# Column-group modulation in the mixers of layer one: two blocks per unit with split contraction, or four blocks per unit with whole contraction

## The chip, the cores and the metric

The kernel runs on one core of a Trainium2 chip. The metric is the device time of one execution in microseconds (us). TensorE (PE) multiplies, ScalarE (ACT) and VectorE (DVE) evict, cast and normalise, SyncE (SP) issues nearly all DMAs, in order, on one queue.

## The reference, cut to what matters

Two layers of a diffusion trunk run over 128 context and 256 denoising tokens. Each layer is modulated by a vector computed from a condition; there are two conditions, one per group of tokens.

```python
mod = jax.nn.silu(cond) @ P['mod_w'][l] + P['mod_b'][l]
sh1, sc1, g1, sh2, sc2, g2 = jnp.split(mod[:, None, :], 6, axis=-1)
h = _rms(x, P['norm1_g'][l]) * (1 + sc1) + sh1
...
x = x + g1 * (merged @ P['w_out'][l])
h = _rms(x, P['norm2_g'][l]) * (1 + sc2) + sh2
```

`mod_w` is 1024 x 6144, so `mod` has 48 blocks of 128 channels: blocks 0 to 15 are `sh1` and `sc1`, 16 to 23 `g1`, 24 to 39 `sh2` and `sc2`, 40 to 47 `g2`. The change concerns blocks 16 to 39 of the first layer, which are needed only after that layer's mixers.

## The kernel before, in words

Weights stay in HBM in pieces of at most 128 x 1024 numbers (512 KB). `raw` (line 179) loads a piece into a tile `wr`; there are four `wr` buffers, shared by all pieces. `split` turns a piece into two rounded halves, `wh` by a cast on ScalarE (line 194) and `wl` by a subtraction on VectorE (line 195), of which there are four and three buffers. The `wr` buffer is free again once the subtraction has read it. Each product is then three matmuls on TensorE (lines 201, 202, 203); two of them need `wh`, one needs `wl`.

A modulation unit (`mod_unit`) uses its pieces as loaded, in full fp32, so their two `wr` buffers are free only when TensorE has read them. Each half of the contraction is one piece of four blocks of 128 rows by 256 columns. Line 362 puts the four row blocks on the four groups of 32 columns of the array, so that the four run side by side and each group of 32 PSUM partitions holds a quarter of the sum. ScalarE copies that out (line 365), TensorE transposes it twice (line 370), VectorE adds the four quarters (372) and the bias (375). In the first layer's mixers 12 such units make blocks 24 to 39 and then 16 to 23.

`dense` yields the projections one by one and calls `unit(1)` between them at 18 places, of which the first 12 issue one unit each. `weave` interleaves the dense part with the attention (`sc`, `ta`, `av`, `tw` tiles) by a count of steps. The tile scheduler then fixes each engine's order before the run; loads are hoisted by a priority of 400 instructions.

Of the kernel before, what the change touches and what calls it, by code (L numbers as in the profile page):

```python
# [17 lines left out]
ALU = mybir.AluOpType  # L18
# [3 lines left out]
P = 128  # L22
D = 1024
KD = 8
# [20 lines left out]
PV = {}  # L45
# [17 lines left out]
AB = 3  # L63


MODS = ((0, 1, 8, 8), (2, 2, 1, 4), (3, 1, 8, 8))


def weight_pieces():

    out = []

    def add(key, name, l, nkb, cols, per):
        for i, k0 in enumerate(range(0, nkb, per)):
            out.append(((l, *key, i), name, l, range(k0, min(k0 + per, nkb)), cols))

    def r(a, n):
        return list(range(a, a + n))

    def mod(l, s):  # L80
        for p in range(MODS[s][3]):
            a = MODS[s][0] * D + MODS[s][1] * p * P
            add(("mod", s, p), "mod_w", l, KD, r(a, P) + r(a + MODS[s][2] * P, P), 4)

    mod(0, 0)
    for l in range(L):
        for i in range(1 if l == 0 else AB):
            add(("u", i), "w_in", l, KD, r(512 + P * i, P) + r(P * i, P), 4)
        for c in range(2):
            for i in range(3):  # L90

                e = r(3200, 32) if (i, c) == (2, 1) else []
                add(("qkv", i, c), "w_in", l, KD, r(1024 + 512 * i + 256 * c, 256) + e, 3 if e else 4)
        add(("c", 0), "w_in", l, KD, r(2560, 256), 4)
        add(("c", 1), "w_in", l, KD, r(2816, 256), 4)
        add(("c", 2), "w_in", l, KD, r(3072, P), 8)
        for i in range(1 if l == 0 else AB, 4):
            add(("u", i), "w_in", l, KD, r(512 + P * i, P) + r(P * i, P), 4)
        for g in range(2):
            add(("uq", g), "w_uq", l, 3, r(384 * g, 384), 2)  # L100
            add(("ukv", g), "w_ukv", l, 2, r(512 * g, 512), 2)
            for i in range(4):
                add(("g", 1 + g, i), "w_in", l, KD, r(3232 + 1024 * (1 + g) + 256 * i, 256), 4)
            for i in range(4):
                n, w = (("od", "w_diff_out"), ("om", "w_mla_out"))[g]
                add((n, i), w, l, 4, r(256 * i, 256), 4)
        if l == 0:
            mod(0, 2)
            mod(0, 1)
        for i in range(4):  # L110
            add(("g", 0, i), "w_in", l, KD, r(3232 + 256 * i, 256), 4)
            add(("oc", i), "w_conv_out", l, 4, r(256 * i, 256), 4)
        for i in range(4):
            add(("wo", i), "w_out", l, KD, r(256 * i, 256), 4)
        for f in range(2):
            for i in range(8):
                add(("up", f, i), "w_up", l, KD, r(2048 * f + 256 * i, 256), 4)
            for i in range(4):
                for j, k0 in enumerate(range(16 * f, 16 * f + 16, 4)):
                    out.append(((l, "dn", f, i, j), "w_down", l, range(k0, k0 + 4), r(256 * i, 256)))  # L120
    return out


PIECES = weight_pieces()
WOFF = {}
_o = 0
# [18 lines left out]
class Body:  # L145
# [204 lines left out]
    def mod_cols(s, p):  # L350

        a, d = MODS[s][0] * KD + MODS[s][1] * p, MODS[s][2]
        return slice(a, a + d + 1, d)

    def mod_unit(self, l, s, p, pool=None):

        V, E = self.V, self.E
        ps = self.psum("mm" if pool is None or p % 2 else "av")
        for h in range(2):
            w, _, n = self.raw((l, "mod", s, p, h), pool)  # L360
            for j in range(4):
                E.matmul(ps[32 * j : 32 * j + 32, :256], self.cond[:, 4 * h + j, :], w[:, j * 256 : j * 256 + 256],  # L362
                         start=h == 0, stop=h == 1, tile_position=(0, 32 * j))
        m = self.tl(pool, [P, 256], "m", 5) if pool else self.slot("tmpA", 256)
        self.A.copy(m, ps[:, :256])

        def rest():
            pt = self.psum("tw")
            for i in range(2):
                E.transpose(pt[:, i * P : i * P + P], m[:, i * P : i * P + P], self.ident)  # L370
            t = self.tl(self.cp, [P, 2, 2], "modt", 2)
            V.tensor_reduce(t, pt[:, : 2 * P].rearrange("p (i j c) -> p i c j", i=2, j=4)[:, :, 0:2, :], AX.X, ALU.add)
            b = self.mod_cols(s, p)
            o = PV["modb"][0]
            V.tensor_tensor(self.modT[l][:, b, :], t, self.pv[l][:, o + b.start : o + b.stop : b.step]
                            .unsqueeze(2).to_broadcast([P, 2, 2]), ALU.add)

        if pool:
            return rest
        self.after(4, rest)  # L380

    def mod_block(self, l, b):
# [818 lines left out]

    def dense(self, l, h, m):

        units = [(s, p) for s in (2, 1) for p in range(MODS[s][3])] if l == 0 else []

        def unit(n):
            for _ in range(n):
                if units:
                    self.mod_unit(0, *units.pop(0))
                    yield 4  # L1210

        yield from self.qkv(l, h, 0)
        yield from self.qkv(l, h, 1)
        yield from self.cproj(l, h)
        todo = list(range(2 if l == 0 else AB, CB))
        yield from self.conv_in(l, todo.pop(0), h)
        yield from unit(1)
        yield from self.mla_q(l, 0)
        for b in todo:
            yield from self.conv_in(l, b, h)  # L1220
            yield from unit(1)
        if l == 0:
            yield from self.mla_kv(l, 0)
        for i in range(4):
            m += yield from self.gate(l, 1, i, h)
            yield from unit(1)
            if l > 0 and i == 0:
                yield from self.mla_kv(l, 0)
            if i == (1 if l == 0 else 2):
                yield from self.mla_q(l, 1)  # L1230
            if i == (2 if l == 0 else 3):
                yield from self.mla_kv(l, 1)
        yield "od1"
        for i in range(4):
            yield from self.branch_out(l, "od", i, self.od, m[2 * i : 2 * i + 2], None)
            yield from unit(1)
        self.flags.add("od")
        gm = []
        for i in range(4):
            gm += yield from self.gate(l, 2, i, h)  # L1240
            yield from unit(1)
        yield "om1"
        self.conv(l)
        for i in range(4):
            yield from self.branch_out(l, "om", i, self.om, gm[2 * i : 2 * i + 2], m)
            if i == 0:
                self.flags.add("z")
            yield from unit(1)
        yield from unit(len(units))
        yield "oc"  # L1250

    def chains(self, l):
# [168 lines left out]
```

## Time and profile before

| | |
|---|---|
| median of 3 runs | 1370.95 us (1370.3 to 1371.1) |
| profiled execution | 1370.67 us |
| its span, first to last instruction | 1368.9 us |
| TensorE busy in the span | 1350.6 us (99%) |
| VectorE, ScalarE busy | 1065.6 us (78%), 686.8 us (50%) |
| mean granted TensorE clock | 0.997 of full speed |
| first layer's mixers with the 12 units | about 150 to 330 us of the span |

The span leaves out 1.8 us around the profiled execution. Busy TensorE time counts each matmul to its modelled end, and neighbours overlap: what a matmul costs is the distance between starts, not its length. A record of an fp32 matmul is one of its two passes, so a unit's 8 matmuls are 16 records; a transpose is one record.

### The profile page before, as it was taken

The page shows a single profiled execution, that of the slowest core. Times are in us where ns is not written, and L with a number is a line of the kernel's source. Part 1 is how long each engine was busy: PE and PEld are TensorE (multiplying, and loading weights), DVE is VectorE, ACT ScalarE, POOL GpSimd, SP SyncE. Part 2 cuts the span into 40 slices and gives each one's busy share as a digit, 9 for nine tenths or more (in the row PEclk, how much of TensorE's full clock was granted, in tenths as well). Part 3 has the DMA queues.
Part 4 walks back from the last instruction along what each step waited for, and adds up shares of the span by engine and source line. Part 5 has one row for each costly group of instructions (what it writes and reads, how often), then busy time and mean ns, then how long its engine had stood idle before and what let it go on. Part 6 is the DMA issues. An engine that isn't in the chain of part 4 may idle for free.

```text
span 1368.9 us, 22037 instructions
## 1 busy us (share of the span) xinstructions
PE 1350.6 (99%) x8192; PEld 1267.4 (93%) x8192; DVE 1065.6 (78%) x2549; ACT 686.8 (50%) x1297; POOL 16.7 (1%) x34
## 2 busy tenths in 40 slices
PE   5999999999999999999999999999999999999998
PEld 3999887879999999999999998988899999999998
DVE  5777998995998999975568779989999897435532
ACT  3556656453544662276336566664544466326621
POOL 0000000000000000000000000000000000000000
PEclk9999999999999999999999999999999999999999
DMA  9523344445574677753444323322257454333341
GB/s 371 172 91 112 121 141 146 138 171 211 157 250 137 202 223 247 240 166 123 149 146 139 104 89 104 93 81 88 80 201 250 147 184 155 124 124 123 126 144 53
DMA packets 62683, 209.46 MB, mean 153 GB/s; under 512 B 7840, under 2 KB 13600, under 8 KB 62320
## 3 DMA queue, kind: packets, MB, share of 16 engines
q1 hardware_dynamic: 56304, 196.93, 43.8%
q0 software_dynamic: 1808, 6.63, 1.5%
q10 hardware_dynamic: 4464, 4.50, 0.9%
q8 instruction: 64, 1.05, 0.3%
q14 instruction: 43, 0.35, 0.1%
HBM read 203.54 MB, written 4.49 MB: 152 GB/s over the span
## 4 chain that ended last, share of the span: by engine, by line
PE 95%; DVE 2%; DMA 1%; ACT 1%; SPq 0%; issue 0%; DVEq 0%
PE mm L201 20%; PE mm L202 19%; PE mm L203 19%; PE sc L202 9%; PE sc L203 9%; PE sc L201 9%; PE sc L755 3%; PE av L967 2%; PE ta L770 1%; PE mm L362 1%; DMA wr<-wts 1%; PE av L822 1%; PE tw L936 1%; DVE wl L195 1%; PE tw L921 0%; ACT wh L194 0%
## 5 line engine op out<-in xcount | busy, mean ns | idle before, releaser
L194 ACT CAST wh<-wr 128x1024 fp32r<-128x1024 f32 (+3 forms) x280 | 289.5, 1035 | 346.0 <-PE mm L202 173.8
L195 DVE TENSOR_TENSOR wl<-wr,wh 128x1024 fp32r<-128x1024 f32 (+3 forms) x280 | 336.6, 1203 | 155.1 <-PE mm L203 67.8
L201 PE MATMUL mm<-h,wh 128*128 128x384 f32 x848 | 293.1, 346 | 0.8 <-ACT wh L194 0.8
L203 PE MATMUL mm<-h,wl 128*128 128x384 f32 x848 | 285.9, 337 | 0.6 <-DVE wl L195 0.6
L202 PE MATMUL mm<-h,wh 128*128 128x384 f32 x592 | 199.6, 337 | 0.3 <-DVE h L435 0.3
L201 PEld LDWEIGHTS mm<-h,wh 128*128 128x128 f32 x848 | 159.4, 188 | 10.8 <-issue 7.2
L203 PEld LDWEIGHTS mm<-h,wl 128*128 128x128 f32 x848 | 159.3, 188 | 1.5 <-DVE wl L195 1.0
L1024 DVE SCALAR_TENSOR_TENSOR z<-u,dwh,z 128x399 f32<-128x399 f32 x240 | 146.8, 627 | 0.3
L390 DVE SCALAR_TENSOR_TENSOR wj<-wm,srow 128x1024 bf16<-128x1024 f32 x112 | 136.5, 1219 | 5.1 <-DMA wm<-modwT 4.6
L203 PE MATMUL sc<-h,wl 128*128 128x384 f32 x336 | 113.1, 337 | 0.0
L202 PEld LDWEIGHTS mm<-h,wh 128*128 128x128 f32 x592 | 111.4, 188 | 1.8 <-DVE h L435 0.6
L201 PE MATMUL sc<-h,wh 128*128 128x384 f32 x336 | 113.0, 336 | 0.0
L202 PE MATMUL mm<-o,wh 128*128 128x384 f32 x320 | 109.2, 341 | 0.0
L203 PE MATMUL mm<-x,wl 128*128 128x386 f32 x288 | 98.0, 340 | 0.0
L202 PE MATMUL mm<-x,wh 128*128 128x386 f32 x288 | 97.4, 338 | 0.0
L201 PE MATMUL mm<-x,wh 128*128 128x386 f32 x288 | 97.0, 337 | 0.0
L203 PE MATMUL sc<-x,wl 128*128 128x386 f32 x272 | 92.5, 340 | 0.0
L202 PE MATMUL sc<-x,wh 128*128 128x386 f32 x272 | 92.0, 338 | 0.0
L201 PE MATMUL sc<-x,wh 128*128 128x386 f32 x272 | 91.4, 336 | 0.0
L1302 ACT ACTIVATE tmp<-tmp 128x128 f32<-128x128 f32 (+1 forms) x128 | 51.6, 448 | 69.0 <-DVE tmp L1300 68.6
L201 PE MATMUL mm<-wh,h 128*128 128x256 f32 (+1 forms) x288 | 85.0, 295 | 0.0
L202 PE MATMUL mm<-wl,h 128*128 128x256 f32 (+1 forms) x288 | 81.9, 285 | 0.0
(267 smaller groups left out, 2649.3 us busy)
## 6 DMA issues: line engine op xcount, KB each, us to landing
wr<-wts SPq DMA_DIRECT2D x306, 512.0 KB, 3.5
wm<-modwT SPq DMA_DIRECT2D x56, 512.0 KB, 4.3
srow<-condrow POOLq DMA_DIRECT2D x2, 1024.0 KB, 7.0
wr<-wts SPq DMA_DIRECT2D x4, 432.0 KB, 3.3
G<-xT SPq DMA_DIRECT2D x8, 192.0 KB, 4.2
wr<-wts SPq DMA_DIRECT2D x4, 384.0 KB, 3.0
G<-xT POOLq DMA_DIRECT2D x8, 192.0 KB, 3.5
xd<-G ACTq DMA_DIRECT2D x8, 192.0 KB, 2.2
```

What stands on the lines that cost most here:

```text
L194: self.A.copy(hi[:, :n], w[:, :n])
L195: self.V.tensor_tensor(lo[:, :n], w[:, :n], hi[:, :n].bitcast(F32), ALU.subtract)
L201: self.E.matmul(ps, ah, bh, start=start, stop=False)
L202: self.E.matmul(ps, ah, bl, start=False, stop=False)
L203: self.E.matmul(ps, al, bh, start=False, stop=stop)
L362: E.matmul(ps[32 * j : 32 * j + 32, :256], self.cond[:, 4 * h + j, :], w[:, j * 256 : j * 256 + 256], start=h == 0, stop=h == 1, tile_posi ...
L390: V.scalar_tensor_tensor(j, w, 0.5, self.srow[:, c, :], ALU.mult, ALU.mult, accum_out=self.modT[l][:, b, c : c + 1])
L755: E.matmul(sc[:, :n], q[c][:, qs], k[c][:, ks], start=True, stop=True)
L770: self.E.transpose(pt[:, j : j + P], e[:, j : j + P], self.ident)
L967: E.matmul(av[64 * i : 64 * i + 64, tt * P : tt * P + P], vm[:, k0 // P + j, hv : hv + 64], eT[i][:, j * P : j * P + P], start=j == 0, sto ...
L1024: self.V.scalar_tensor_tensor(z[b], self.u[:, b, k : k + ZW], self.dw[:, b * CK + k : b * CK + k + 1], z[b], ALU.mult, ALU.add)
L1302: A.activation(r[:, s:e], r[:, s:e], AF.Relu, bias=r[:, T + c : T + c + 1])
```

## The change

The 12 units of two blocks become 6 of four blocks (`mod_quad`). A unit's four pieces each hold two row blocks for 4 x 128 columns. Each group of 32 array columns now belongs to one block and accumulates all eight row blocks, in 32 matmuls of 128 columns (before: 16 of 256 for as many blocks). So one 128 x 128 copy and one transpose remain per unit; VectorE adds the bias in two instructions and no longer adds quarters. `unit(1)` issues a unit at every other place and then yields 8 steps, not 4. A unit holds all four `wr` buffers.

```diff
--- before.py
+++ after.py
@@ -63,7 +63,15 @@
 AB = 3
 
 
-MODS = ((0, 1, 8, 8), (2, 2, 1, 4), (3, 1, 8, 8))
+MODS = ((0, 1, 8, 8),)
+
+QUADS = ((16, 2, 2), (24, 8, 4))
+
+
+def quad_blocks(s, p):
+    a, d, _ = QUADS[s]
+    a += (4 if d == 2 else 2) * p
+    return [a, a + 1, a + d, a + d + 1]
 
 
 def weight_pieces():
@@ -81,6 +89,11 @@
         for p in range(MODS[s][3]):
             a = MODS[s][0] * D + MODS[s][1] * p * P
             add(("mod", s, p), "mod_w", l, KD, r(a, P) + r(a + MODS[s][2] * P, P), 4)
+
+    def quad(l, s):
+        for p in range(QUADS[s][2]):
+            cols = [c for b in quad_blocks(s, p) for c in r(b * P, P)]
+            add(("quad", s, p), "mod_w", l, KD, cols, 2)
 
     mod(0, 0)
     for l in range(L):
@@ -105,8 +118,8 @@
                 n, w = (("od", "w_diff_out"), ("om", "w_mla_out"))[g]
                 add((n, i), w, l, 4, r(256 * i, 256), 4)
         if l == 0:
-            mod(0, 2)
-            mod(0, 1)
+            quad(0, 1)
+            quad(0, 0)
         for i in range(4):
             add(("g", 0, i), "w_in", l, KD, r(3232 + 256 * i, 256), 4)
             add(("oc", i), "w_conv_out", l, 4, r(256 * i, 256), 4)
@@ -377,6 +390,33 @@
 
         if pool:
             return rest
+        self.after(4, rest)
+
+    def mod_quad(self, l, s, p):
+
+        V, E = self.V, self.E
+        ps = self.psum("mm")
+        for i in range(4):
+            w, _, n = self.raw((l, "quad", s, p, i))
+            for k in range(2):
+                for j in range(4):
+                    o = k * 512 + j * P
+                    E.matmul(ps[32 * j : 32 * j + 32, :P], self.cond[:, 2 * i + k, :], w[:, o : o + P],
+                             start=i + k == 0, stop=i + k == 4, tile_position=(0, 32 * j))
+        m = self.slot("tmpA", P)
+        self.A.copy(m, ps[:, :P])
+
+        def rest():
+            pt = self.psum("tw")
+            E.transpose(pt[:, :P], m, self.ident)
+            b = quad_blocks(s, p)
+            o = PV["modb"][0]
+            t = pt[:, :P].rearrange("p (j c) -> p j c", j=4)[:, :, 0:2]
+            for i in range(2):
+                c = slice(b[2 * i], b[2 * i] + 2)
+                V.tensor_tensor(self.modT[l][:, c, :], t[:, 2 * i : 2 * i + 2, :], self.pv[l][:, o + c.start : o + c.stop]
+                                .unsqueeze(2).to_broadcast([P, 2, 2]), ALU.add)
+
         self.after(4, rest)
 
     def mod_block(self, l, b):
@@ -1201,13 +1241,15 @@
 
     def dense(self, l, h, m):
 
-        units = [(s, p) for s in (2, 1) for p in range(MODS[s][3])] if l == 0 else []
+        units = [(s, p) for s in (1, 0) for p in range(QUADS[s][2])] if l == 0 else []
+        turn = [0]
 
         def unit(n):
             for _ in range(n):
-                if units:
-                    self.mod_unit(0, *units.pop(0))
-                    yield 4
+                turn[0] += 1
+                if units and turn[0] % 2:
+                    self.mod_quad(0, *units.pop(0))
+                    yield 8
 
         yield from self.qkv(l, h, 0)
         yield from self.qkv(l, h, 1)
@@ -1246,7 +1288,7 @@
             if i == 0:
                 self.flags.add("z")
             yield from unit(1)
-        yield from unit(len(units))
+        yield from unit(2 * len(units))
         yield "oc"
 
     def chains(self, l):
```

Where instructions stand is shown at three places; the first two are the fourth new unit (`wr_3250` to `wr_3280`). SP's queue before, around the unit at the same place (`wr_3241`, `wr_3247`); the brackets name whom a load waits for, PE being TensorE:

```order
L179 DMA wr_3241<-wts 128x1024 [waits DMAHW3_49,PE_49]
L179 DMA wr_3247<-wts 128x1024 [waits DMAHW1_49,DVE_49,Activation_49]
L179 DMA wr_3263<-wts 128x1024 [waits DMAHW7_49,PE_49]
L179 DMA wr_3311<-wts 128x1024 [waits DMAHW0_49,PE_49]
L179 DMA wr_3317<-wts 128x1024 [waits DMAHW4_49,DVE_49]
```

and of the change, from the unit's first piece on:

```order
L192 DMA wr_3250<-wts 128x1024 [waits DMAHW6_49,DVE_49]
L192 DMA wr_3260<-wts 128x1024 [waits DMAHW7_49,DVE_49]
L192 DMA wr_3270<-wts 128x1024 [waits DMAHW0_49,DVE_49]
L192 DMA wr_3280<-wts 128x1024 [waits DMAHW1_49,DVE_49,Activation_49]
L192 DMA wr_3304<-wts 128x1024 [waits DMAHW2_49,PE_49]
L192 DMA wr_3353<-wts 128x1024 [waits DMAHW3_49,PE_49]
L192 DMA wr_3414<-wts 128x1024 [waits DMAHW4_49,PE_49]
L192 DMA wr_3424<-wts 128x1024 [waits DMAHW5_49,PE_49]
```

Before, the next weight piece, `wr_3263`, waits for the unit ahead of this one; now the next piece, `wr_3304`, stands behind the unit's own four pieces and waits for TensorE to read the first of them.

TensorE before, at the unit; `wh_3265` and `wl_3266` come from `wr_3263`:

```order
L936 MATMUL tw_3232<-ident_94,tok_3004 96x128 x2
L362 MATMUL mm_3240<-wr_3241,cond_73 32x256 x4
L362 MATMUL mm_3240<-wr_3247,cond_73 32x256 x4
L201 MATMUL mm_3261<-o_1640,wh_3265 128x384
L202 MATMUL mm_3261<-o_1641,wh_3265 128x384
L203 MATMUL mm_3261<-o_1640,wl_3266 128x384
L370 MATMUL tw_3255<-ident_94,tmpA_3253 128x128 x2
L201 MATMUL mm_3261<-o_1654,wh_3265 128x384
L202 MATMUL mm_3261<-o_1655,wh_3265 128x384
```

and of the change; `wh_3306` comes from `wr_3304`:

```order
L404 MATMUL mm_3249<-wr_3250,cond_73 32x128 x8
L404 MATMUL mm_3249<-wr_3260,cond_73 32x128 x8
L404 MATMUL mm_3249<-wr_3270,cond_73 32x128 x8
L404 MATMUL mm_3249<-wr_3280,cond_73 32x128 x8
L789 MATMUL sc_3318<-kT_3169,qT_2912 128x128 x2
L411 MATMUL tw_3292<-ident_94,tmpA_3290 128x128
L795 MATMUL sc_3381<-kT_3169,qT_2912 128x384
L976 MATMUL tw_3296<-ident_94,tok_2945 96x128 x2
L976 MATMUL tw_3296<-ident_94,tok_3040 96x128 x2
L214 MATMUL mm_3302<-o_1640,wh_3306 128x384
L215 MATMUL mm_3302<-o_1641,wh_3306 128x384
L214 MATMUL mm_3303<-o_1640,wh_3306 128x384
```

Products of the next piece followed the unit at once; now small rows of the attention stand between, and the two products with `wh` of both output tiles are drawn ahead of the first one with `wl`.

The third place is the fifth new unit, which stands where the ninth stood. TensorE before, from that unit on, which attention rows interrupt once:

```order
L362 MATMUL mm_3405<-wr_3406,cond_73 32x256 x4
L362 MATMUL mm_3405<-wr_3412,cond_73 32x256 x3
L770 MATMUL ta_3394<-ident_94,e_3353 128x128 x3
L362 MATMUL mm_3405<-wr_3412,cond_73 32x256
L967 MATMUL av_3339<-eT_3392,v_2897 64x128
L755 MATMUL sc_3434<-kT_3121,qT_2917 128x384
L370 MATMUL tw_3420<-ident_94,tmpA_3418 128x128 x2
L967 MATMUL av_3339<-eT_3398,v_2897 64x128
```

and of the change, from the last piece of the fifth unit on; four more such `av` rows and then the next piece's first product follow:

```order
L404 MATMUL mm_3413<-wr_3444,cond_73 32x128 x8
L810 MATMUL ta_3460<-ident_94,e_3388 128x128 x3
L795 MATMUL sc_3480<-kT_3169,qT_2912 128x384
L411 MATMUL tw_3456<-ident_94,tmpA_3454 128x128
L810 MATMUL ta_3466<-ident_94,e_3390 128x128 x3
L1007 MATMUL av_3376<-eT_3464,v_2944 64x128
L795 MATMUL sc_3483<-kT_3169,qT_2912 128x384
L1007 MATMUL av_3376<-eT_3470,v_2944 64x128
```

The unit is no longer interrupted, and more attention rows stand between the unit and the next piece's first product than at any other of the six places.

## Rows read from the trace of the kernel before

**Rows 1.** The page: busy time by engine, and the chain that ended last.

```profile
PE 1350.6 (99%) x8192; PEld 1267.4 (93%) x8192; DVE 1065.6 (78%) x2549; ACT 686.8 (50%) x1297; POOL 16.7 (1%) x34
...
PE 95%; DVE 2%; DMA 1%; ACT 1%; SPq 0%; issue 0%; DVEq 0%
```

**Rows 2.** Two stretches: busy us of PE, PEld, DVE, ACT, POOL; PEclk; DMA.

```profile
150.00:200.00 50.00, 49.97 (x319) 43.66 (x315) 49.37 (x167) 28.64 (x62) 0.00 (x0) 1.00 0.45 147
...
250.00:290.00 40.00, 40.00 (x288) 31.20 (x288) 36.49 (x89) 17.99 (x40) 0.00 (x0) 1.00 0.50 174
```

**Rows 3.** TensorE around one whole unit: start us, us, what.

```profile
174.96 0.33 PE L202 MATMUL mm<-h,wh 128*128 128x384 f32 x1
175.13 0.34 PE L203 MATMUL mm<-h,wl 128*128 128x384 f32 x1
175.40 1.07 PE L362 MATMUL mm<-wr,cond 128*32 128x256 f32 x16
176.40 0.50 PE L201 MATMUL mm<-wh,cq 128*128 128x512 f32 x1
...
176.97 0.39 PE L203 MATMUL mm<-wh,cq 128*128 128x512 f32 x1
177.20 0.38 PE L370 MATMUL tw<-ident,tmpA 128*128 128x128 f32 x2
177.33 0.48 PE L201 MATMUL mm<-wh,cq 128*128 128x512 f32 x1
```

**Rows 4.** Instructions of L362, 60 to 330 us: ns min/median/max.

```profile
L362 PE MATMUL mm<-wr,cond x192: 379/379/403, 157.2 to 316.7; 128*32 128x256 f32 x192
```

**Rows 5.** That unit's start, L362 alone: busy us (count) of PE, PEld.

```profile
175.30:175.50 0.20, 0.10 (x4) 0.10 (x8) 1.00 0.00 0
```

**Rows 6.** TensorE around an interrupted unit, columns as in rows 3.

```profile
203.55 0.62 PE L362 MATMUL mm<-wr,cond 128*32 128x256 f32 x2
204.10 0.64 PE L936 MATMUL tw<-ident,tok 128*96 128x128 f32 x4
```

**Rows 7.** Chain that ended last, 200 to 235 us: start, us, what.

```profile
217.08 0.33 PE ta L770 x3
...
228.67 0.80 PE av L967 x10
...
234.01 0.65 PE sc L755 x2
```

**Rows 8.** All engines, one load that waited for a unit: release to use.

```profile
261.45 1.07 PE L362 MATMUL mm<-wr,cond 128*32 128x256 f32 x16
...
262.15 7.37 SPq L179 DMA_DIRECT2D wr<-wts  x5
...
265.92 1.05 ACT L194 CAST wh<-wr 128x1024 fp32r<-128x1024 f32 x1 [2.95 <-DMA wr<-wts]
...
267.00 1.23 DVE L195 TENSOR_TENSOR wl<-wr,wh 128x1024 fp32r<-128x1024 f32 x1 [0.20 <-ACT wh L194]
...
270.84 0.44 PE L201 MATMUL mm<-o,wh 128*128 128x384 f32 x1
```

**Rows 9.** Three loads issued in a row (L179).

```profile
DMA to landing us min/median/max: 3.6/4.4/5.1
```

**Rows 10.** All loads of L179 from 150 to 330 us.

```profile
DMA to landing us min/median/max: 3.2/3.8/8.3
```

**Rows 11.** ScalarE's casts by shape, 150 to 330 us: busy us, mean ns.

```profile
L194 ACT CAST wh<-wr 128x1024 fp32r<-128x1024 f32 x27 | 28.3, 1049 | 23.1 <-DMA wr<-wts 12.2 <-PE mm L202 10.1 <-ACT e L762 0.7
...
L194 ACT CAST wh<-wr 128x768 fp32r<-128x768 f32 x1 | 0.8, 835 | 2.2 <-DMA wr<-wts 2.2
```

**Rows 12.** VectorE's subtraction of full pieces, 150 to 330 us.

```profile
L195 DVE TENSOR_TENSOR wl<-wr,wh 128x1024 fp32r<-128x1024 f32 x25 | 30.5, 1220 | 8.0 <-PE mm L203 5.0 <-PE mm L202 1.4 <-issue 1.0
```

**Rows 13.** Windows, columns as in rows 2: clock after waits for loads.

```profile
16.20:19.60 3.40, 1.61 (x12) 0.35 (x10) 1.42 (x6) 1.01 (x3) 0.00 (x0) 1.00 1.02 419
19.60:23.00 3.40, 3.32 (x26) 0.89 (x26) 2.05 (x7) 1.27 (x4) 0.00 (x0) 0.50 1.03 420
```

## Prediction

> **What bounds the kernel now.** I began with the page: TensorE is busy for 99% of the span and makes up 95% of the chain that ended last [rows 1]. Busy time hides small gaps, since neighbouring matmuls overlap, so the stretch of the change comes next: from 150 to 330 us TensorE is busy throughout, at full clock, with VectorE nearly full at first (49.4 of 50 us) and less so later [rows 2]. Distances between starts in the timeline tell what each thing on TensorE costs [rows 3]. I therefore count every microsecond that the change takes from TensorE as won and every one in which TensorE would wait as lost; ScalarE and VectorE matter where TensorE would wait for them.
>
> **What it removes from TensorE.** A whole unit starts at 175.40; the product ahead of it started at 175.13, and such products start 0.17 us apart, so TensorE was free at 175.30. The next product starts at 176.40, and as the first behind a unit is recorded 0.11 us longer than a later one (0.50 against 0.39), the unit costs 1.2 us [rows 3]. Four interruptions by attention rows each add some 0.55: a part of two records lasts until 204.10, 0.55 us from 203.55, with about 0.1 ahead of it, where its share of a whole unit is about 0.1 [rows 6]. A pair of transposes costs from 177.20 to 177.33 and 0.1 of a longer record, 0.25; I take 0.28, as some stand after an fp32 neighbour [rows 3]. Before: 12 x 1.2 + 4 x 0.55 + 12 x 0.28 = 20.0 us.
>
> **What it puts there.** In a unit 16 records go four at a time. Its 1.07 us less one record's 0.379 leave 0.69 us for three further rounds, 0.23 each, the first somewhat longer; 0.215 is the 256 columns in two clocks each at the full 2.4 GHz [rows 3, 4]. The rounds of the changed unit have 128 columns, and this shape is not in the trace. Below, half of 0.215; above, 0.215, if the weight loads set the pace. The nearest row is a run of fp32 transposes with as many columns and four times the weights: three take 0.33 on the chain, 0.11 each [rows 7]. I take 0.11. A unit then costs 16 x 0.11 and the 0.35 that the old one has besides its four rounds (1.2 less 0.86), 2.1 us. Six such, one interruption (the third unit keeps one) and six single transposes at 0.28 less 0.11 make 12.6 + 0.55 + 1.0 = 14.2 us. TensorE is relieved of **5.8 us**.
>
> A rule speaks against half-length rounds. The Trainium skill ("TensorE: Matmul & The Clock Gate", Part 3, The mechanism) says that weight loads overlap with running matmuls only where the row group differs; here all four groups use the same 128 rows. The trace differs: in the first 0.1 us of a unit eight loads were under way beside four matmuls, so the second round's loads go beside the first round's matmuls [rows 5]. By the rule the relief would be gone, by the row it stands.
>
> **What it adds: a wait behind each unit.** The four pieces of a unit fill all four `wr` buffers, and in SP's order the load of the next weight piece then waits for TensorE to read the first of the four. Before, two buffers went on serving weights. What that chain takes is shown once in the trace, at the unit of 261.45: the load that its first piece held back is issued at 262.15, 0.70 after the unit's first matmul; its cast starts at 265.92 and the subtraction ends 1.23 after 267.00, at 268.23 [rows 8]. So `wh` is there 5.5 us after the unit's first matmul and `wl` 6.8. This load was the first of two and the piece was first wanted at 270.84, 2.6 us later: nothing was lost. With the first of three landing 3.6 us after issue [rows 9], the cast at 1.05 and the subtraction at 1.22 [rows 11, 12] I take 5.4 and 6.7. Below: landing at 3.2, the shortest seen [rows 10], 5.0 and 6.2. Above: the cast and subtraction late by one neighbour each, 6.5 and 8.5. The first read of the changed unit is as long, four rounds of 0.11 and one tail against two of 0.23 and one tail.
>
> TensorE's cover for this wait is the unit itself (2.0 up to its exit) and what its order holds between unit and first product with `wh`. Priced at 0.11 a transpose or 128-column record, 0.65 for a 384-wide `sc`, 0.16 for an `av` of 64 columns (ten records take 0.80) [rows 7] and 0.17 a product, in the order of the units:
>
> First: five transposes and six 128-wide `av` records, 11 x 0.11 = 1.2; cover 3.2. Its next piece is 768 wide (landing 3.2, cast 0.84 [rows 10, 11]): `wh` at 4.8, wait 1.6. Second: seven `tw`, two `sc` of 128 and 384, 1.6; cover 3.6, wait 1.8. Third: its interruption falls within the first piece, so counted from the resumption the buffer is freed at 0.5 and `wh` is there at 5.1; cover 1.7 for the rest of the unit and 1.9 for seven transposes, two `sc` of 128 and one of 384, wait 1.5, and after three 512-wide products (0.22 each) another 0.6 for `wl`. Fourth: five transposes, two `sc` of 128 and one of 384, 1.65; cover 3.65, wait 1.75, and after four products 0.6 for `wl`. Fifth: seven transposes, two `sc`, six `av`, 3.0; cover 5.0, wait 0.4, and then 0.4, since the order draws two products of the second piece forward, whose cast ends 1.05 later. Sixth: seven transposes, two `sc`, one `av`, 2.2; cover 4.2, wait 1.2. Together **9.85 us**. With the lower bounds at all six it is about 7.6, with the upper ones about 17. A stall lets ScalarE and VectorE catch up, but TensorE waited for neither, so nothing returns; it is late for everything behind it to the end.
>
> **Costed at nothing.** The copies on ScalarE and the additions on VectorE become fewer. TensorE's next steps do not wait for them; should VectorE be behind at the first two units, its 0.6 us convolution steps ahead of a subtraction would add up to about 1 us, which is in the upper bound. The bytes loaded are the same, 24 pieces of 512 KB. The single `tw` bank is held by the one transpose in the shadow of the wait; without that cover an addition of some 0.3 us per unit would show.
>
> **Sum.** 1370.67 - 5.8 + 9.85 = 1374.7 for an execution like the profiled one; the median of the runs stands 0.28 above it. **Forecast: 1375.0 us**, 0.3% slower.
>
> **The rivals.** *The refill is quick enough* (faster). The place is the same six; if the next piece's `wh` came 3.9 us or less after the unit's first matmul, the waits would sum to less than 3 us and the relief would win; with no wait at all 1370.95 - 5.8 = 1365.2. For it: pieces were always ready before use in these mixers [rows 8]. Against it: no landing was under 3.2 [rows 10], and with release and cast that is 5.0. Half the waits, from longer attention rows than I priced, would give 1370.1. *The rounds do not shorten.* Then each unit costs 1.7 us more, but that time also covers the wait, which falls to some 2.8 in all as the first buffer is freed only 0.3 later: 1370.95 - 5.8 + 10.2 + 2.8 = 1378.2. The Trainium skill's rule, above, is the ground for it; the loads beside the first round are against it [rows 5]. *The clock falls.* In the first modulation stretch TensorE was busy for 1.61 of 3.40 us, waiting for loads, and the granted clock in the following 3.40 us was 0.50, the 1.2 GHz level [rows 13]; such a stretch delays by 1.7 us. Stalls of 1.5 to 2.4 us beside light rows may do the same; two to four times make 1378.4 to 1381.8. Against it, TensorE here is dense on either side of the wait.
>
> **How the numbers follow.** A change of 0.2%, 2.7 us, is about what this kernel's measurement can tell from none; the bounds are 1368.2 and 1373.7. My sum, with 1 us either way for the rounds and 0.3 for each wait, 1372.2 to 1378: chance 0.50, of which 0.07 is below 1373.7. Clock: 0.12. Rounds: 0.09. Waits about half: 0.16, all within 0.2%. Waits nearly gone: 0.13, faster. Slower: 0.43 + 0.12 + 0.09 = 0.64; same: 0.07 + 0.16 = 0.23; faster 0.13. The bounds of the waits alone reach from 1372.7 to 1382. The range for 8 in 10 takes in the case of half the waits and leaves out most of the fast case and the worst of the clock and of the waits: 1368.0 to 1380.5.
>
> **What would show it.** After: L404's 32 matmuls in 1.9 to 2.2 us (rounds); one transpose each; and, decisive, TensorE idle six times in front of a first product, 0.4 to 2 us, with the cast of a piece as releaser and that piece's load issued 0.7 us after the unit's start. Wrong would be: no idle there, or loads issued ahead of the unit's first matmul; or a granted clock below 1 between 150 and 330 us.

## The result, and the profile after

The change is slower: 1381.08 us (median of 6 runs, 1377.38 to 1385.37) against 1370.57 us for the kernel before in the same comparison (6 runs, 1368.9 to 1371.1), a ratio of 1.0083 with a 95% interval of 1.0070 to 1.0095. The direction is the forecast's; the size is not: 10.5 us where 4.4 was forecast against this median, and the time lies above the stated range, which ended at 1380.5. The profiled execution took 1382.72 us, its span is 1380.9 us.

Three things are to be read in the profile after: what a unit costs, where TensorE waits, and the clock.

The page, busy time by engine and the chain that ended last (answers to [rows 1]); TensorE's busy time is 1.2 us less than before in a span that is 12 us longer:

```profile
PE 1349.4 (98%) x8366; PEld 1274.7 (92%) x8366; DVE 1065.2 (77%) x2537; ACT 684.4 (50%) x1291; POOL 16.7 (1%) x34
...
PE 91%; DVE 4%; DMA 2%; ACT 1%; SPq 1%; issue 0%; DVEq 0%; ACTq 0%
```

The windows of [rows 2], in the same columns: TensorE, idle there for 0.03 us at most before, now is for 4.8 and 1.9 us, and the granted clock of the first window has fallen to 0.93:

```profile
150.00:200.00 50.00, 45.22 (x345) 40.62 (x347) 45.32 (x158) 25.63 (x58) 0.00 (x0) 0.93 0.36 110
250.00:290.00 40.00, 38.07 (x335) 32.08 (x333) 38.33 (x114) 15.54 (x38) 0.00 (x0) 1.00 0.32 109
```

All engines around the fourth unit, in the timeline (start us, us, what, and in brackets the idle time ahead of it and who ended it; answers to [rows 3, 8]):

```profile
269.74 0.34 PE L216 MATMUL mm<-o,wl 128*128 128x384 f32 x1
...
270.01 1.95 PE L404 MATMUL mm<-wr,cond 128*32 128x128 f32 x64
...
270.71 6.29 SPq L192 DMA_DIRECT2D wr<-wts  x5
...
274.34 1.04 ACT L207 CAST wh<-wr 128x1024 fp32r<-128x1024 f32 x1 [2.05 <-DMA wr<-wts]
...
275.42 1.23 DVE L208 TENSOR_TENSOR wl<-wr,wh 128x1024 fp32r<-128x1024 f32 x1
...
275.44 0.44 PE L214 MATMUL mm<-o,wh 128*128 128x384 f32 x1 [1.64 <-ACT wh L207]
...
276.70 0.44 PE L216 MATMUL mm<-o,wl 128*128 128x384 f32 x1 [0.28 <-DVE wl L208]
```

This is the chain of the forecast, link by link. Counted from the unit's first matmul, the load of the next piece goes out at 0.70 us, the cast starts at 4.33, `wh` is there at 5.4 (forecast 5.4) and `wl` at 6.65 (forecast 6.7), and TensorE stands still in front of both. The unit itself is as short as forecast: 64 records within 1.95 us. One record lasts 0.27 (the median of line 404), so the remaining 1.68 us are 15 further rounds of 0.11.

TensorE's waits from 150 to 345 us by releaser, all there are (who waited for whom: us in total, times, longest):

```profile
PE mm L214 <- ACT wh L207: 4.1, 3, 2.0
PE av L862 <- ACT eT L812: 2.6, 1, 2.6
PE tw L411 <- ACT tmpA L407: 1.1, 1, 1.1
PE tw L976 <- DVE tok L943: 0.9, 1, 0.9
PE mm L214 <- ACT tok L901: 0.8, 1, 0.8
PE tw L411 <- ACT kT L977: 0.8, 1, 0.8
PE tw L961 <- ACT qT L962: 0.7, 1, 0.7
PE mm L215 <- DVE wl L208: 0.4, 1, 0.4
PE mm L216 <- DVE wl L208: 0.3, 1, 0.3
PE ta L810 <- DVE modT L417: 0.2, 1, 0.2
```

The first line is the wait that was forecast, for the cast of the next piece, and the two for `wl` are its second part. The waits in front of transposes for `tok` (0.9) and `kT`, behind the second unit, and `qT`, behind the third, name another releaser. But the second unit starts at 198.35, and its next piece's cast and first product are these:

```profile
202.65 1.05 ACT L207 CAST wh<-wr 128x1024 fp32r<-128x1024 f32 x1 [0.34 <-DMA wr<-wts]
...
203.76 0.68 PE L214 MATMUL mm<-h,wh 128*128 128x384 f32 x1
```

`wh` is there at 203.70, 5.35 us after the unit's first matmul, and the product follows at once: the idle time ahead of it, 1.6 us where 1.8 was forecast, has the length that the cast gives it, whoever is named.

What the forecast did not have stands behind the first unit. The largest wait, ahead of `av`, in the timeline of TensorE, ScalarE and SP's queue:

```profile
156.06 13.62 SPq L192 DMA_DIRECT2D wr<-wts  x9
...
165.99 0.34 PE L216 MATMUL mm<-wh,cq 128*128 128x384 f32 x1
167.03 1.04 ACT L207 CAST wh<-wr 128x1024 fp32r<-128x1024 f32 x1 [1.90 <-DMA wr<-wts]
...
168.39 0.47 ACT L812 COPY eT<-ta 128x384 f32<-128x384 f32 x1
...
168.91 1.03 PE L862 MATMUL av<-v,eT 128*128 128x128 f32 x6 [2.58 <-ACT eT L812]
```

ScalarE's order has a cast ahead of the copy `eT`. That cast waits 1.90 us for its load, which like all loads behind the first unit is late; its own piece is first wanted at 183.3. TensorE needs the copy at 166.3 and gets it 2.6 us later: the held buffers reach TensorE through ScalarE's queue, by way of a piece that nobody needs yet. The wait for the other `tok` (0.8, ahead of a product at 170.78) stands right behind this one.

The wait of 1.1 us for `tmpA`, the unit's own copy, has another cause: ScalarE's order has an exponential `e` ahead of that copy, and it waits for VectorE, which is nearly full there.

```profile
157.23 0.67 ACT L802 ACTIVATE e<-sc,nm,qsc 128x384 f32<-128x384 f32 x1 [2.21 <-DVE nm L798]
...
158.54 0.26 ACT L407 COPY tmpA<-mm 128x128 f32<-128x128 f32 x1
...
158.85 0.33 PE L411 MATMUL tw<-ident,tmpA 128*128 128x128 f32 x1 [1.06 <-ACT tmpA L407]
```

The clock, in the windows behind that stall (columns as in [rows 2]; the two that start at 203.70 and 316.40 are the other half-clock stretches):

```profile
166.20:169.60 3.40, 0.82 (x7) 0.69 (x6) 2.46 (x3) 2.58 (x4) 0.00 (x0) 1.00 0.93 287
169.60:173.00 3.40, 2.56 (x10) 2.27 (x9) 3.30 (x11) 3.23 (x9) 0.00 (x0) 0.50 0.72 236
173.00:176.40 3.40, 3.40 (x13) 3.40 (x12) 2.24 (x15) 0.03 (x1) 0.00 (x0) 0.50 0.02 8
176.40:179.80 3.40, 3.40 (x21) 3.23 (x20) 1.93 (x6) 1.65 (x3) 0.00 (x0) 0.99 0.00 0
...
203.70:207.20 3.50, 3.50 (x16) 3.35 (x15) 3.25 (x4) 2.53 (x4) 0.00 (x0) 0.51 0.55 184
316.40:319.80 3.40, 3.40 (x16) 2.63 (x16) 3.26 (x5) 3.36 (x7) 0.00 (x0) 0.50 0.61 214
```

TensorE was busy for 0.82 of 3.40 us; in the next 6.8 us the granted clock is 0.50, its 1.2 GHz level. The two full windows at 173.00 and 176.40 hold 13 and 21 matmuls. The other two stretches also follow units, the second and the sixth; in the 3.4 us ahead of them TensorE was busy for 1.77 and 1.46. What the level costs is seen in the starts of the products, 0.31 us apart here and 0.17 at full clock [rows 3]:

```profile
173.19 0.53 PE L215 MATMUL mm<-h,wh 128*128 128x384 f32 x1
173.50 0.53 PE L216 MATMUL mm<-h,wl 128*128 128x384 f32 x1
```

**A stretch that can be compared.** All kernels have the same two marks on TensorE, matmuls with `ones` that begin a norm's statistics: one ahead of the first unit, one behind the first layer's mixers and everything that the units can move. Before and after, in the timeline:

```profile
145.47 0.72 PE L697 MATMUL tw<-ones,z 128*128 128x1 f32 x6
...
440.56 0.61 PE L322 MATMUL tw<-ones,z 128*128 128x1 f32 x5
```

```profile
143.59 0.72 PE L737 MATMUL tw<-ones,z 128*128 128x1 f32 x6
...
452.71 0.50 PE L335 MATMUL tw<-ones,z 128*128 128x1 f32 x4
```

From mark to mark it is 295.1 us before and 309.1 after, 14.0 more; the second mark is 928.3 and 928.2 us ahead of the end of the span. The first mark came 1.9 us earlier in the profile after; it lay anywhere from 143.2 to 146.7 us in the profiles of this study, so that part is not the change's. 1370.67 + 14.0 - 1.9 = 1382.8, the profiled execution's 1382.72. The experiments below are read by this stretch too, since it leaves the start out.

### The profile page after: what moved, and what is told of

Its sections match the earlier page's. It is cut to its first block, busy times and chain, and to the rows that moved or that the text cites. A ratio compares the mean times of both kernels' runs of the same rounds, so it can differ in the third digit from the quotient of the medians.

```text
span 1380.9 us, 22360 instructions
## 1 busy us (share of the span) xinstructions
PE 1349.4 (98%) x8366; PEld 1274.7 (92%) x8366; DVE 1065.2 (77%) x2537; ACT 684.4 (50%) x1291; POOL 16.7 (1%) x34
## 4 chain that ended last, share of the span: by engine, by line
PE 91%; DVE 4%; DMA 2%; ACT 1%; SPq 1%; issue 0%; DVEq 0%; ACTq 0%
PE mm L214 19%; PE mm L215 19%; PE mm L216 19%; PE sc L215 9%; PE sc L216 9%; PE sc L214 8%; PE sc L795 3%; DMA wr<-wts 2%; PE av L1007 2%; PE ta L810 1%; DVE z L1064 1%; DVE wl L208 1%; PE av L862 1%; ACT wh L207 1%; PE tw L976 1%; PE tw L693 0%
## 5 line engine op out<-in xcount | busy, mean ns | idle before, releaser
L214 PEld LDWEIGHTS mm<-h,wh 128*128 128x128 f32 x848 | 161.1, 190 | 12.5 <-issue 6.4
L215 PEld LDWEIGHTS mm<-h,wh 128*128 128x128 f32 x592 | 113.0, 191 | 1.7 <-issue 0.7
```

Of the source, the lines that this page charges most:

```text
L214: self.E.matmul(ps, ah, bh, start=start, stop=False)
L215: self.E.matmul(ps, ah, bl, start=False, stop=False)
```

## The experiments

In the table, "stretch" is the time from mark to mark, "idle" what TensorE was idle from 150 to 360 us (210 less its busy time in that window), and "half clock" the time at a granted clock of 0.50 between 150 and 345 us, all of the profiled execution. Times are medians, with the ratio to the kernel before in the same comparison and its 95% interval. The kernel before had 1370.57, 1370.30, 1370.14 and 1369.57 us in the four comparisons, so that differences of medians across them are good to about 1 us, and the ratios go before them. Two expectations put the change's waits at about 14 us; by this column they are 12.0.

| kernel | median us | ratio | stretch | idle | half clock |
|---|---|---|---|---|---|
| before | 1370.57 | 1 | 295.1 | 0.1 | 0 |
| after | 1381.08 | 1.0083 [1.0070, 1.0095] | 309.1 | 12.0 | 13.7 |
| no units | 1352.81 | 0.9874 [0.9857, 0.9890] | 277.8 | 0.1 | 0 |
| pairs of old units | 1379.41 | 1.0071 [1.0058, 1.0085] | 304.1 | 9.4 | 0 |
| new format, old size | 1368.37 | 0.9988 [0.9979, 0.9997] | 293.3 | 0.2 | 0 |
| before, fewer `v`, `kT` | 1370.21 | 0.9999 [0.9991, 1.0008] | 295.1 | 0.1 | 0 |
| after, two own buffers | 1367.88 | 0.9984 [0.9975, 0.9993] | 293.3 | 1.1 | 0 |
| after, one own buffer | 1372.04 | 1.0022 [1.0013, 1.0030] | 297.5 | 4.7 | 0 |
| two own buffers, even places | 1368.76 | 0.9993 [0.9984, 1.0002] | 293.8 | 1.7 | 0 |
| after, ten fills | 1381.29 | 1.0085 [1.0069, 1.0101] | 306.6 | 4.5 | 0 |
| after, five fills | 1377.16 | 1.0063 [1.0050, 1.0076] | 303.6 | 6.0 | 3.4 |
| after, from 3rd place | 1381.95 | 1.0085 [1.0070, 1.0100] | 308.8 | 9.9 | 13.7 |
| the same, ten fills | 1381.67 | 1.0082 [1.0067, 1.0098] | 306.3 | 3.9 | 0 |
| after, even places | 1386.78 | 1.0128 [1.0114, 1.0143] | 309.9 | 16.3 | 10.2 |

**Is it the held buffers?** The theory was that TensorE waits because a unit holds all four `wr` buffers; the rival, that the new format of the unit is dear. In one kernel the last two pieces of each unit go into two buffers of their own; for the space `v` and `kT` have two buffers each in place of three, and a control has only that.

```diff
-            w, _, n = self.raw((l, "quad", s, p, i))
+            w, _, n = self.raw((l, "quad", s, p, i), self.ap if i > 1 else None)
...
-        w = self.tl(pool or self.wp, [P, PIECE], "wr", 8 if pool else 4)
+        w = self.tl(pool or self.wp, [P, PIECE], "wr", (2 if pool is getattr(self, "ap", None) else 8) if pool else 4)
```

> The change, but the last two of a unit's four pieces go into two buffers of their own, so that a unit holds two of the four shared piece buffers; room for them is made by two instead of three buffers for v and for kT of the attention. Held buffers (the loss comes from the four held buffers, directly and through the clock): no first product of a piece waits behind a unit, clock 1.00 from 150 to 330 us, the relief of about 6 us stands: 1364 to 1367 us, plus what fewer v and kT buffers cost (control). Format (the loss comes from the new column groups or from the larger, rarer units): 1377 us or more, as the change.

> Control: the kernel before, with two instead of three buffers for v and for kT of the attention. Both theories: within 0.2% of before, 1368 to 1373 us, if these buffers only let the attention run ahead; any difference is to be taken off the run with two own buffers.

Measured: 1367.88 us, 13.2 less than the change and 0.16% less than before, above the 1364 to 1367 expected, as the relief is smaller than reckoned (below); the control is as before. TensorE's waits of 150 to 345 us, all there are:

```profile
PE tw L411 <- ACT tmpA L407: 0.6, 1, 0.6
PE ta L810 <- ACT eT L812: 0.2, 1, 0.2
PE ta L810 <- DVE e L996: 0.2, 1, 0.2
```

The waits for `wh`, for `tok` and for `eT` ahead of `av` are gone together, and so are the half-clock stretches. Of the wait for `tmpA` 0.6 us are left: at least that part does not come from the four held buffers. With one own buffer (`i > 2` in the first line of the diff) the effect has a middle value:

> The kernel with own buffers, but for the last piece of a unit only, so that a unit holds three of the four shared buffers and one goes on serving weights. Theory (it is the held set that makes TensorE wait): most waits go, since the next piece's load no longer stands behind the unit, but the piece after it does: 1368.5 to 1372 us. Rival (it takes two free buffers to be rid of the wait): 1374 to 1378 us. If the buffers were not the cause: 1380 us or more.

1372.04 us, at the upper bound of what was expected (1372): one buffer that goes on serving weights removes 7.3 of the 12.0 us that TensorE idles, the second another 3.6.

The counterpart puts the hold into the kernel before: its old units, two directly behind one another at every other place, so that four buffers are held.

```diff
+        turn = [0]
...
-                if units:
-                    self.mod_unit(0, *units.pop(0))
-                    yield 4
+                turn[0] += 1
+                if units and turn[0] % 2:
+                    self.mod_unit(0, *units.pop(0))
+                    self.mod_unit(0, *units.pop(0))
+                    yield 8
...
```

> The kernel before with its old units of two blocks, but two of them one directly behind the other at every second place (and 8 steps yielded), so that four piece buffers are held at once in the old format. Held buffers: waits of about 14 us and half-clock stretches as in the change, without its relief beyond about 1 us: 1382 to 1392 us. Format: nothing of the new column groups is in it: 1369 to 1373 us.

1379.41 us, below the 1382 to 1392 expected and without the half-clock stretches that were expected too, but 9.1 us above its kernel before, and with the same kinds of waits. Of its nine groups the first three; the largest wait is again for a copy on ScalarE (`tok`), not for a cast:

```profile
PE mm L201 <- ACT tok L861: 2.3, 1, 2.3
PE mm L201 <- ACT wh L194: 1.9, 3, 0.9
PE tw L370 <- DVE peg L580: 1.0, 1, 1.0
...
```

And the new format without the hold: units of two blocks at the old places, rounds of 128 columns, one transpose. The part of the edit that makes the matmuls:

```diff
-                E.matmul(ps[32 * j : 32 * j + 32, :256], self.cond[:, 4 * h + j, :], w[:, j * 256 : j * 256 + 256],
-                         start=h == 0, stop=h == 1, tile_position=(0, 32 * j))
...
+                for i in range(2):
+                    g = 32 * (2 * (j % 2) + i)
+                    E.matmul(ps[g : g + 32, :P], self.cond[:, 4 * h + j, :], w[:, j * 256 + i * P : j * 256 + i * P + P],
+                             start=h == 0 and j < 2, stop=h == 1 and j > 1, tile_position=(0, g))
```

> The kernel before with the new format at the old size: units of two blocks and two pieces at the old places, each column group taking one block and every second row block in 128-column matmuls, one copy and one transpose per unit. Held buffers: two buffers held as before, no new wait; 8 rounds of 0.11 and 0.35 are the old 1.2 us, one transpose less each, so 12 x 0.11 = 1.3 us gained: 1368 to 1370.5 us. Format: if 128-column rounds or their order cost, slower than before, 1373 us or more.

1368.37 us, as expected, with 0.2 us of waits. So the format is not dear; the hold is.

**What are the units worth?** This kernel leaves out the modulation of blocks 16 to 39 of the first layer, with zeros in its place.

```diff
-        units = [(s, p) for s in (2, 1) for p in range(MODS[s][3])] if l == 0 else []
+        units = []
+        if l == 0:
+            self.V.memset(self.modT[l][:, 16:40, :], 0.0)
```

> The kernel before without the modulation of blocks 16 to 39 of the first layer (left out: those loads, matmuls, copies, transposes and additions; zeros in their place). A floor for any version of these units: by the account of 20.0 us for the units on TensorE before, 1350.5 us, between 1349 and 1352. If loads and other engines also count, lower: 1345 to 1349; if part of the units lies in gaps that TensorE has anyway, 1352 to 1358.

1352.81 us: above the first expectation, in the range that was given for units which lie in part in gaps. The stretch is 277.8 us, 17.3 less than with the old units, where the forecast's account had 20.0. The new units, in the kernel with two own buffers, take 293.3 - 277.8 less 1.1 idle, 14.4 us, where the account had 14.2. The relief is 2.9 us, not 5.8.

With these two numbers every stretch can be added up: 277.8, plus 14.4 for new or 17.3 for old units, plus idle. That leaves +0.6 us with one own buffer, -0.2 with own buffers at even places, and -0.4 for the pairs, all kernels that held the clock in the stretch. For the change it leaves 309.1 - 277.8 - 14.4 - 12.0 = 4.9 us: the clock is left for it. The starts of TensorE's matmuls agree. Of the 42 distances between starts in the change's half-clock stretches, 37 have their like, with the same neighbours, at full clock, and without idle time they are 4.2 us longer in all than these; the other five last 1.4 us together, and half of that would make 4.9.

**Is it the clock?** If the falls of the clock cost what is left over, matmuls that do nothing but keep TensorE busy in the waits should pay. Behind each unit ten, and in another kernel five, go into columns of the unit's PSUM tile that nobody reads. They are as wide as the products that start 0.17 us apart [rows 3].

```diff
         self.A.copy(m, ps[:, :P])
+        f = self.fill[0][0]
+        for _ in range(10):
+            E.matmul(ps[:, P:512], f[:, :P], f[:, :T], start=True, stop=True)
...
+        self.fill = h
```

> The change, and behind each unit ten matmuls of 128x384 into columns of the unit's PSUM tile that nobody reads: about 1.7 us of extra work on TensorE for each unit, 10 us in all, put where TensorE would wait. The waits themselves are as long, so what fill the wait hides costs nothing. Theory 1 (the waits make the granted clock fall, and the fall costs some 4 us or more beyond the waits): no stretch at half clock between 180 and 330 us, and the time falls in spite of the added work or at least does not rise: 1376 to 1381 us. Rival (the clock costs nothing beyond the waits, or falls for another reason): the clock falls as often as in the change, and the time rises by the fill that finds no wait to hide in: 1382 to 1388 us.

> The kernel with extra matmuls, with five behind each unit instead of ten (about 0.85 us each unit, 5 us in all). If ten hid fully in the waits, five do as well, the granted clock stays at 1.00 between 150 and 330 us, and the time is that of the kernel with ten, 1380 to 1382 us. If ten partly lengthened the stretch, five take 1 to 4 us less, 1377 to 1380 us. If five are too few to keep the clock up, stretches at half clock as in the change, and 1380 to 1384 us.

With ten, no half clock is left in the stretch, and the sum closes without a clock term: 306.6 - 277.8 - 14.4 - 4.5 idle leaves 9.9 us, which is about the 60 fills at 0.17. The whole time, 1381.29 us, is that of the change and 0.3 above what was expected: the fill took the place of idling and of the clock's loss. With five the kernel is 3.9 us faster than the change by the medians and 0.2%, 2.7 us, by the ratios, and its stretch 5.5 us shorter, though it has 30 matmuls, 5 us, more to do. The two ratios' intervals overlap (1.0070 to 1.0095, 1.0050 to 1.0076), so the runs alone only suggest it; the traces show where it comes from. The same stall of the first unit is still there, and behind it the one half-clock stretch that is left; behind the second and sixth unit the clock now holds (windows of the kernel with five):

```profile
166.20:169.70 3.50, 1.19 (x8) 0.86 (x7) 3.50 (x6) 3.21 (x8) 0.00 (x0) 1.00 0.89 300
169.70:173.10 3.40, 3.40 (x12) 3.40 (x11) 3.40 (x17) 1.96 (x5) 0.00 (x0) 0.50 0.55 174
...
203.80:207.20 3.40, 3.40 (x22) 3.35 (x22) 3.40 (x8) 2.63 (x8) 0.00 (x0) 1.00 0.84 257
316.40:319.80 3.40, 3.31 (x21) 3.02 (x20) 2.05 (x4) 1.60 (x4) 0.00 (x0) 1.00 0.87 306
```

Its sum leaves 303.6 - 277.8 - 14.4 - 6.0 = 5.4 us, 0.3 more than its 30 fills at 0.17, for 3.4 us at half clock. So what is left in such a sum is good to about 1 us.

**Is the first place special?** The first unit's stalls suggested moving the units: to the 3rd, 5th, ... 13th place, with and without fill, or to the even places.

```diff
-                if units and turn[0] % 2:
+                if units and turn[0] > 1 and turn[0] % 2:
```

```diff
-                if units and turn[0] % 2:
+                if units and turn[0] % 2 == 0:
```

> The change with the first of the 18 places skipped, so that its six units stand at the 3rd, 5th, ... 13th place; nothing is left out. Theory 1 (the first unit is dear because it stands where ScalarE is behind, and its queue holds a cast that waits for a load ahead of a copy that TensorE needs): the two stalls of 2.8 and 1.1 us after the first unit are gone, each unit has an ordinary wait of 0.5 to 2.1 us, and fewer stretches at half clock follow: 1374 to 1378 us, 3 to 7 us less than the change. Rival (the place is of no account; a held set of four buffers costs as much anywhere): 1380 to 1383 us, with a stall of over 2.5 us elsewhere.

> Both: units from the 3rd place on, and the ten extra matmuls behind each. With both theories right: granted clock 1.00 from 150 to 330 us, the six waits filled: the time of the late-start kernel less what half clock still costs there, plus the fill that finds no wait, 1374 to 1379 us. If the clock is of no account: 2 to 5 us above the late-start kernel without fill.

> The change with its six units at the 2nd, 4th, ... 12th place instead of the 1st, 3rd, ... 11th; nothing is left out and no unit stands behind the last place of before. Theory 1 (the first place costs more than the others, since ScalarE is behind there and a cast that waits for a load stands ahead of a copy that TensorE needs): no stall above 2.3 us in the mixers, six ordinary waits of 0.4 to 2.1 us, 8 to 11 us together instead of 14.4: 1375 to 1378.5 us. Rival (the hold costs as much wherever the first unit stands): 1380 to 1383 us.

> The kernel with two own buffers for a unit's last two pieces, with the units at the 2nd, 4th, ... 12th place. With no waits left, the floor without units (1352.8) and 14.3 us for the units give 1367.1 us; expected 1366.5 to 1368.5, no more than 1 us from the same kernel with units at the odd places (1367.9). If the place still matters without the hold, outside of that.

The time went against the theory: 1381.95 us from the 3rd place, in the rival's range, and 1386.78 at the even places, above both ranges. The stall of 2.6 us ahead of `av` is gone in both, but the last unit now stands at the end of the mixers. TensorE at the last unit, at the even places:

```profile
318.52 1.95 PE L404 MATMUL mm<-wr,cond 128*32 128x128 f32 x64
320.86 0.33 PE L411 MATMUL tw<-ident,tmpA 128*128 128x128 f32 x1 [0.39 <-ACT tmpA L407]
323.44 0.80 PE L335 MATMUL tw<-ones,z 128*128 128x1 f32 x6 [2.25 <-DVE z L357]
329.13 0.69 PE L214 MATMUL mm<-h,wh 128*128 128x384 f32 x1 [4.89 <-ACT wh L207]
```

Behind it there is nothing but the norm's statistics to cover with, and the next piece's `wh` comes 10.6 us after the unit's first matmul: 7.5 us in three waits. Its load, issued at 319.23, was slow: a load of 1 MB (`srow`) had gone out on another queue at 318.45, and from 320 to 328 us the DMA engines were busy for 0.81 to 1.00 of the time. In the change that load goes out at 327.8, behind all the holds. So the price of a hold does depend on the place, by what covers it and by what else is loading, but these kernels do not test the first place alone, since each moved the last unit too. With own buffers the places differ by 0.9 us (0.9984 and 0.9993, intervals overlap; 1368.76 is 0.3 above its expected range). Fill in the late kernel again removed the half clock and left the time unchanged, above the 1374 to 1379 expected. The sums of the two kernels without fill leave 6.7 us from the 3rd place, with 13.7 at half clock, and 1.4 at the even places, where TensorE idled for 4.9 of the 10.2.

## What the prediction had right, and which steps failed

The direction came from the right mechanism: held buffers, late loads, TensorE waiting. The size was wrong, and so was the account behind it, by a sign that the forecast had named itself: the granted clock fell below 1 between 150 and 330 us. Undoing the hold alone brings the change from 1381.1 to 1367.9 us, putting it alone into the old units costs 9 us. By the forecast's own terms, of which the clock failed by most:

- **The relief, forecast 5.8 us, measured 2.9.** The new side was right (14.2; measured 14.4), and with it the 0.11 us a round, which was a choice between two bounds. The Trainium skill's rule ("TensorE: Matmul & The Clock Gate", Part 3, The mechanism), by which weight loads overlap with running matmuls only where the row group differs, does not agree with this trace either: 16 rounds on the same rows, each with four loads, took 1.95 us, and loads were under way for 1.69 of them. The step that failed is "12 x 1.2 + 4 x 0.55 + 12 x 0.28 = 20.0": without the units the stretch is only 17.3 shorter. Each unit was charged with all distances at its edges, and 2.7 us of these remain when it is gone. In the trace before, only 11 of the 24 items (12 units, 12 pairs of transposes) stand alone between products; the others stand beside attention rows, whose own edges to the products stay. That fits, but what it amounts to was not measured.
- **The waits, forecast 9.85 us, measured 12.0 of idle time** in the profiled execution. Up to the next piece, chain and cover came out within 0.8 us of the forecast: from the first unit to the sixth 1.3, 1.6, 1.7, 1.9, 0 and 1.95 us were idle, 8.5 together, where 1.6, 1.8, 2.1, 2.35, 0.8 and 1.2 were forecast. That the first unit's is near is in part luck, as 1.1 of its 1.3 us are the wait for `tmpA` behind VectorE. The other 3.4 us, for `eT` and then `tok` behind the first unit, the forecast did not have. The step that failed was "TensorE's next steps do not wait for them" of ScalarE's copies: the copy `eT` stood behind a cast that waited 1.90 us for its load, the copy `tmpA` behind an exponential that waited 2.21 us for VectorE. "TensorE idle six times in front of a first product" held for three.
- **The clock, taken at 1.00 in the sum, costs about 4.9 us** in the profiled execution, worked out as what is left of the stretch, and 4.2 to 4.9 by the starts; with five fills per unit the stretch is 5.5 us shorter. The forecast had this as a rival with the right mechanism and the right rows [rows 13], at 1378.4 to 1381.8 us, which holds the median, at 1.7 us for each 3.4 at half clock, where 4.9 in 13.7 us make 1.2. It was given 0.12 only, for "TensorE here is dense on either side of the wait". That was no reason: TensorE is dense before 166 us, and one wait of 2.6 us with a few matmuls beside it was followed by 6.8 us at half clock.

Together: 1370.67 - 2.9 + 12.0 + 4.9 - 1.9 (the earlier first mark) = 1382.8. These sizes are those of the profiled execution, and its stretch, 14.0 us longer than before, is above the 10.5 between the medians; the change's runs spread over 8 us, and what each lost to waits and clock is known of this one alone. Of the other rivals, a refill quick enough falls with the load of 270.71, and rounds that do not shorten with the unit of 1.95 us.

## What to carry to other kernels

Before work is gathered into larger units, count the buffers that a unit holds against the pool it shares: what it saves is a sum of small edges, 2.9 us here, and a unit that holds all of them costs more, 12.0 us of waits and some 4.9 by the clock, while two buffers of its own make the same change a small gain (0.16%). A late load is not paid only by the piece that it brings: look at what stands behind its cast in the in-order queue of the engine that casts. And measure what an item costs by taking it out of a run, not by adding up distances at its edges, where a term decides the sign.

## What the runs showed of the hardware

A kernel that does 30 matmuls more for nothing, in waits of TensorE, was no slower, by the medians 3.9 us and by the ratios 2.7 us faster (the intervals overlap), with 3.4 instead of 13.7 us at half clock in its profile. A wait of 2.3 us was followed by half clock there, a wait as long in the pairs of old units was not. In the change's six runs the mean granted clock was 0.991 to 0.998, and the slowest run (1385.37) has the lowest, the two at 0.995 and 0.994 took 1382.72 and 1383.96, and the three at 0.996 and above 1377.38 to 1379.43.
